# Result banks held as persistent tiles, and a new place for the whole-array blocks among the transpositions

## The chip, the cores and the metric

The kernel runs on one core of a Trainium2 chip. The metric is the device time of one execution in microseconds, the median of several. A ratio is the mean time of one kernel's fast runs over that of the other's of the same rounds, so it is not quite the ratio of the medians that stand beside it.

## The reference

```python
B, S, D, H = 64, 1024, 1024, 16         # Dh = D // H = 64
route_logits = x @ route_w              # (B, S, 16)
best_head = np.argmax(route_logits, axis=-1)
x_heads = x.reshape(B, S, H, Dh)
for h in range(H):
    mask = (best_head == h)
    out[:, :, h, :] = np.matmul(x_heads[:, :, h, :], experts[h]) * mask[:, :, None]
```

Everything is float32. x has 268 MB and out as many: each row is read once and written once, and all but one of its 16 heads is zero in the result.

## The kernel before

The engines are called PE (matrix multiplication; PEld is its loading of weights), ACT, DVE and POOL (work on elements) and SP (which issues loads and stores). SBUF and PSUM are memories on the chip; PE writes its results to banks of PSUM here.

The 65536 rows are cut into 512 tiles of 128 rows, and the loop takes them in pairs. For each tile,

- eight transpositions on PE put x into two PSUM banks (ps_t), four a bank, and ACT copies each bank to SBUF (xt);
- a *split pass* of 40 small matmuls on PE (blocks 0 to 4 of a row, on quarters of the array) writes banks 0 and 1 of a three-bank result tile (ps_e), and ACT copies these two banks to SBUF (raw);
- three *whole-array blocks* (two matmul instructions each) write bank 2 of the same tile;
- DVE reduces the logits out of all three banks, finds the best head, makes the mask, and multiplies bank 2 by it into the output row (ot); POOL multiplies raw by the mask into the rest; SP stores the row.

The kernel holds eight PSUM banks: two for ps_t, and two result tiles of three. A pair's split passes come first; then a string, ORDER, says how the pair's six whole-array blocks (F) are mixed with the 16 transpositions (T) of the next pair.

```python
ORDER = "FTFTFTTTFTFTFTTTTTTTTT"
# ... (cut)
ps_t_pool = ctx.enter_context(tc.tile_pool(name="ps_t", bufs=2, space=bass.MemoryType.PSUM))
ps_e_pool = ctx.enter_context(tc.tile_pool(name="ps_e", bufs=2, space=bass.MemoryType.PSUM))
# ... (cut: constants, load, transposes)

def split_pass(ps, xt):                       # L123: 40 matmuls into banks 0 and 1
    for p in range(NS):
        # ... (cut: half, th)
                    nc.tensor.matmul(ps[th * 64:(th + 1) * 64, half, o0:o0 + W], lhsT=..., rhs=..., ...)
    raw = raw_pool.tile([P, 2, SLOTS * STEP], FP32, name="raw", tag="raw")
    nc.scalar.copy(out=raw[:, :, 0:RW], in_=ps[:, 0:2, 0:RW])        # L130
    return raw

def whole_block(ps, xt, f):                   # L135: bank 2
    nc.tensor.matmul(ps[:, 2, o0:o0 + STEP], lhsT=xt[:, NS + f, :], rhs=mf[:, f, :], ...)

def finish(j, ps, raw):
    parts = ps[:, :, 0:SLOTS * STEP].rearrange("k b (s w) -> k b s w", w=STEP)
    nc.vector.tensor_reduce(out=lg, in_=parts[:, :, :, Dh:W]..., op=ALU.add, axis=AX.XY)   # L142
    # ... (cut: max, max_index, mask)
    nc.vector.tensor_tensor(out=ov[:, NS:], in1=bc(mk[:, NS:]), op=ALU.mult,
                            in0=ps[:, 2, W:W + NF * STEP]...)        # L160, "the multiply"
    # ... (cut: two products on POOL, L168)
    nc.sync.dma_start(out=og[j], in_=ot)

for j in range(-2 * AHEAD, NT + 2, 2):        # manual schedule: engines run in this order
    # ... (cut: loads of 12 tiles ahead)
    pair = [i for i in (j - 2, j - 1) if i >= 0]
    for i in pair:
        ps = ps_e_pool.tile([P, SLOTS, HB], FP32, name="ps_e", tag="ps_e")
        work[i] = (ps, split_pass(ps, xts[i]))
    # ... (cut: tr = the 16 transpositions of tiles j, j + 1)
    for step in order:                        # "T": next(tr); "F": whole_block, and finish
        # ... (cut)                           # after a tile's third
```

## Time and profile before

| | before |
|---|---|
| time, median of 3 | 1503.12 us (1500.57 to 1503.49) |
| PE busy, share of the span | 94% |
| ACT, DVE, POOL busy | 64%, 51%, 48% |
| period: start of one pair's split passes to the next's | 5.75 us median, 5.79 us mean |
| HBM traffic over the span | 359 GB/s |

From the page of the kernel before: busy times of the engines; and of the slices of the span the DMA line (tenths of the time that the DMA engines were busy) and the GB/s they moved.

```profile
PE 1404.1 (94%) x27648; PEld 1231.4 (82%) x27648; DVE 757.4 (51%) x3074; ACT 960.2 (64%) x1537; POOL 721.7 (48%) x1031
...
DMA  9999999999999999999999999999999999999994
GB/s 355 405 365 368 365 367 360 371 369 369 361 361 369 362 371 362 369 360 375 367 365 363 367 367 365 366 360 370 365 361 368 365 363 366 366 368 366 364 350 185
```

The DMA line looks full from start to end, but the GB/s line below it has a slice of 405 among slices of 360 to 375, so busy time is not a measure of what is left. The windows (length in us, busy time and count of each engine, granted clock, DMA share, GB/s) show the same:

```profile
core 0: us, PE busy (x) PEld busy (x) DVE busy (x) ACT busy (x) POOL busy (x), PEclk, DMA share, GB/s
25.00:60.00 35.00, 32.95 (x659) 28.91 (x652) 17.59 (x73) 22.45 (x37) 16.75 (x25) 1.00 1.03 415
300.00:340.00 40.00, 37.63 (x754) 32.98 (x753) 20.20 (x82) 25.67 (x42) 19.71 (x28) 1.00 1.00 372
```

DMA share 1.03 goes with 415 GB/s, and 1.00 with 372. The Trainium skill says it too (Perfetto Trace Analysis, "Identifying the Most-Contended Engine"): for DMA, judge by bandwidth, since 16 engines make occupancy misleading. There was room.

The timeline of one period (start and length in us, engine, line, what, count; in brackets the idle time just before and what ended it):

```profile
700.49 1.89 PE L123 MATMUL ps_e<-mv,xt 64*64 64x80 f32 x80
...
700.76 0.56 DVE L160 TENSOR_TENSOR ot<-ps_e,mask 128x384 f32<-128x384 f32 x1
...
701.43 0.79 PEld L123 LDWEIGHTS ps_e<-mv,xt 64*64 64x64 f32 x40 [0.18 <-ACT xt L114]
...
704.71 0.71 PE L112 MATMUL ps_t<-ident,xin 128*128 128x128 f32 x5
...
705.01 1.08 ACT L114 COPY xt<-ps_t 128x512 f32<-128x512 f32 x2 [0.59 <-PE ps_t L112]
...
705.65 0.66 PE L112 MATMUL ps_t<-ident,xin 128*128 128x128 f32 x4 [0.24 <-ACT xt L114]
```

Two places lose time. The nine transpositions at the end of ORDER are five and then, after a stop, four (705.65): the last four need the ps_t bank whose ACT copy runs from 705.01. And the 80 matmuls of the two split passes, shown as one row, hold a stop at 701.43, where the weight loads (PEld) of the second pass begin. The multiply of the tile that used this ps_e buffer before ends at 701.31 (700.76 and 0.56 are rounded).

The list of waits (us in total, times, longest) blames something else for the second:

```profile
PE ps_t L112 <- ACT xt L114: 64.2, 256, 3.1
...
PEld ps_e L123 <- ACT xt L114: 49.8, 252, 0.5
...
PE ps_t L112 <- DMA xin<-in_x_dram: 4.4, 1, 4.4
```

The second row gives the 49.8 us to an ACT copy. That copy had ended at 701.18, and the semaphore that the waiting instruction names is counted up by DVE: a wait for several semaphores is put down to whichever came last by the profile, and here the profile chose wrongly. The third row is the only wait of PE for a load.

### The profile page before, as it was taken

What the parts mean: (1) busy time and instruction counts of PE and PEld (TensorE: products, weight loads), DVE (VectorE), ACT (ScalarE), POOL (GpSimd) and SP (SyncE); (2) the same over time, 40 slices, a digit from 0 to 9 for tenths busy, and PEclk for the clock granted to TensorE, in tenths of its full rate; (3) what the DMA queues carried; (4) which work ended last, traced back from release to release, by engine and by line L of the source; (5) the groups of instructions that cost most, each with busy time, mean ns of one, the idle gap of its engine ahead of it and who ended that gap; (6) DMA issues with size and microseconds to landing.
All of it is one profiled execution on the core that took longest, in us unless ns stands there. A gap on an engine that the chain in (4) does not pass through costs nothing. (4 is left out here: it accounts for less than half of the span.)

```text
span 1498.0 us, 66591 instructions
## 1 busy us (share of the span) xinstructions
PE 1404.1 (94%) x27648; PEld 1231.4 (82%) x27648; DVE 757.4 (51%) x3074; ACT 960.2 (64%) x1537; POOL 721.7 (48%) x1031
## 2 busy tenths in 40 slices
PE   7999999999999999999999999999999999999997
PEld 6888888888888888888888888888888888888886
DVE  3454545454545555545555555545454545454544
ACT  5666666666666666666666666666666666666665
POOL 3454544444444545444545454545444444444444
PEclk9999999999999999999999999999999999999999
DMA  9999999999999999999999999999999999999994
GB/s 355 405 365 368 365 367 360 371 369 369 361 361 369 362 371 362 369 360 375 367 365 363 367 367 365 366 360 370 365 361 368 365 363 366 366 368 366 364 350 185
DMA packets 149949, 541.52 MB, mean 361 GB/s; under 512 B 18576, under 2 KB 18576, under 8 KB 149648
## 3 DMA queue, kind: packets, MB, share of 16 engines
q1 hardware_dynamic: 147456, 536.94, 96.5%
q8 instruction: 219, 3.59, 1.0%
q10 hardware_dynamic: 2192, 0.33, 0.1%
q14 instruction: 82, 0.67, 0.1%
HBM read 268.76 MB, written 268.44 MB: 359 GB/s over the span
## 5 line engine op out<-in xcount | busy, mean ns | idle before, releaser
L168 POOL TENSOR_TENSOR ot<-raw,mask 128x384 f32<-128x384 f32 (+1 forms) x1024 | 720.9, 725 | 772.1 <-ACT xt L114 682.7
L112 PE MATMUL ps_t<-ident,xin 128*128 128x128 f32 x4096 | 755.5, 277 | 68.6 <-ACT xt L114 64.2
L114 ACT COPY xt<-ps_t 128x512 f32<-128x512 f32 x1024 | 576.9, 587 | 362.7 <-PE ps_t L112 362.4
L112 PEld LDWEIGHTS ps_t<-ident,xin 128*128 128x128 f32 x4096 | 499.6, 141 | 129.3 <-ACT xt L114 124.9
L135 PE MATMUL ps_e<-mf,xt 128*128 128x144 f32 x3072 | 602.1, 296 | 1.0 <-ACT raw L130 0.7
L123 PE MATMUL ps_e<-mv,xt 64*64 64x80 f32 x20480 | 475.9, 234 | 17.3 <-DVE ot L160 4.9
L135 PEld LDWEIGHTS ps_e<-mf,xt 128*128 128x128 f32 x3072 | 462.9, 191 | 34.7 <-ACT raw L130 1.9
L130 ACT COPY raw<-ps_e 128x704 f32<-128x704 f32 x512 | 382.0, 746 | 159.4 <-PE ps_e L123 159.2
L123 PEld LDWEIGHTS ps_e<-mv,xt 64*64 64x64 f32 x20480 | 399.6, 133 | 95.4 <-ACT xt L114 49.8
L142 DVE TENSOR_REDUCE lg<-ps_e 128x16 f32<-128x144 f32 x512 | 155.0, 303 | 624.5 <-PE ps_e L135 616.3
L160 DVE TENSOR_TENSOR ot<-ps_e,mask 128x384 f32<-128x384 f32 x512 | 285.4, 558 | 19.5 <-DVE mask L150 1.5
L150 DVE TENSOR_SCALAR mask<-hid,ix 128x16 f32<-128x16 f32 x512 | 119.9, 234 | 55.9 <-POOL ot L168 1.8
L146 DVE MAX8 mx<-lg 128x8 f32<-128x16 f32 x512 | 91.2, 178 | 17.7
L148 DVE FIND_INDEX8 ix<-mx,lg 128x8 uint32<-128x16 f32 x512 | 86.5, 169 | 0.0
L148 DVE MATCH_VALUE_LOAD ix<-mx,lg 128x8 f32 x512 | 47.1, 92 | 17.6
L114 ACT ACT_TABLE_LOAD x1 | 1.3, 1283 | 7.5 <-DMA mf<-in_experts_dram 7.5
L79 DVE MEMSET mf<- 128x432 f32 x1 | 0.4, 418 | 0.9 <-PEq L220 0.9
masks.py:197 POOL MEMSET ident<- 128x128 f32 x1 | 0.2, 205 | 0.3 <-POOLq L220 0.3
masks.py:199 POOL TENSOR_SCALAR_AFFINE_SELECT ident<-ident 128x128 f32<-128x128 f32 x1 | 0.3, 294 | 0.0
L220 POOL MEMSET const-float32-0.0<- 128x1 f32 x1 | 0.1, 99 | 0.2 <-issue 0.2
L97 POOL IOTA hid_i<- 128x16 int32 x1 | 0.1, 142 | 0.0
L99 DVE CAST hid<-hid_i 128x16 f32<-128x16 int32 x1 | 0.2, 152 | 0.0
(3 smaller groups left out, 0.3 us busy)
## 6 DMA issues: line engine op xcount, KB each, us to landing
xin<-in_x_dram SPq DMA_DIRECT2D x512, 512.0 KB, 7.3
out_dram<-ot SPq DMA_DIRECT2D x512, 512.0 KB, 5.8
mv<-in_experts_dram ACTq DMA_DIRECT2D x2, 48.0 KB, 5.0
mf<-in_experts_dram ACTq DMA_DIRECT2D x2, 48.0 KB, 3.6
mv<-in_experts_dram ACTq DMA_DIRECT2D x2, 32.0 KB, 3.5
mv<-in_route_w_dram ACTq DMA_DIRECT2D x1, 24.0 KB, 4.2
mf<-in_route_w_dram ACTq DMA_DIRECT2D x1, 24.0 KB, 7.5
mv<-in_route_w_dram ACTq DMA_DIRECT2D x1, 16.0 KB, 2.8
```

Of the source, the lines that this page charges most:

```text
L79: nc.vector.memset(mf, 0.0)
L112: nc.tensor.transpose(ps_t[:, q, :], xin[:, p * P:(p + 1) * P], ident)
L114: nc.scalar.copy(out=xt[:, half * (NB // 2):(half + 1) * (NB // 2), :], in_=ps_t)
L123: nc.tensor.matmul(ps[th * 64:(th + 1) * 64, half, o0:o0 + W], lhsT=xt[half * 64:(half + 1) * 64, p, th * 64:(th + 1) * 64], rhs=mv[half * ...
L130: nc.scalar.copy(out=raw[:, :, 0:RW], in_=ps[:, 0:2, 0:RW])
L135: nc.tensor.matmul(ps[:, 2, o0:o0 + STEP], lhsT=xt[:, NS + f, :], rhs=mf[:, f, :], start=(f == 0), stop=(f == NF - 1), skip_group_check=True)
L142: nc.vector.tensor_reduce(out=lg, in_=parts[:, :, :, Dh:W].rearrange("k b s h -> k h b s"), op=ALU.add, axis=AX.XY)
L146: nc.vector.max(out=mx, in_=lg)
L148: nc.vector.max_index(out=ix, in_max=mx, in_values=lg)
L150: nc.vector.tensor_scalar(out=mask, in0=hid, scalar1=ix[:, 0:1], scalar2=None, op0=ALU.is_equal)
L160: nc.vector.tensor_tensor(out=ov[:, NS:], in1=bc(mk[:, NS:]), op=ALU.mult, in0=ps[:, 2, W:W + NF * STEP].rearrange("k (f w) -> k f w", w=S ...
L168: nc.gpsimd.tensor_tensor(out=ov[:, ab:NS:2], in0=rv4[:, 0:n, :, o0:o0 + Dh], in1=bc(mk[:, ab:NS:2]), op=ALU.mult)
```

## The change

The intent: with the result tiles allocated once and used in turn, banks 0 and 1 should become free for the next split pass without waiting for the multiply, which reads bank 2 alone. That should allow the blocks, which delay the multiply when they come late, to move behind the first four transpositions.

```diff
-ORDER = "FTFTFTTTFTFTFTTTTTTTTT"
+ORDER = "TTTTFTFTFTTFTFTFTTTTTT"
@@
-    ps_e_pool = ctx.enter_context(tc.tile_pool(name="ps_e", bufs=2, space=bass.MemoryType.PSUM))
+    ps_e_pool = ctx.enter_context(tc.tile_pool(name="ps_e", bufs=1, space=bass.MemoryType.PSUM))
@@
+    ps_es = [ps_e_pool.tile([P, SLOTS, HB], FP32, name=f"ps_e{i}", tag=f"ps_e{i}") for i in range(2)]
@@
         for i in pair:
-            ps = ps_e_pool.tile([P, SLOTS, HB], FP32, name="ps_e", tag="ps_e")
+            ps = ps_es[i % 2]
             work[i] = (ps, split_pass(ps, xts[i]))
```

## The prediction

> **What bounds it now.** A pair of tiles takes 5.75 us (median distance between starts of the split passes; mean 5.79). The page has PE busy 94%, ACT 64%, DVE 51%, POOL 48%. The slices show DMA at nine tenths all along, but it is not the limit yet: loads run 12 tiles ahead, the waits show PE waiting for one once (4.4 us), and at 25 to 60 us, with a backlog of mixed loads and stores, the windows show 415 GB/s against 372 at 300 to 340 us. PE's in-order chain sets the pace, and loses 0.7 us a period in two places (timeline, 699.9 to 706.3 us):
>
> 1. The last four transpositions wait for a ps_t bank: a gap of 0.51 us instead of 0.11. The eighth transposition comes late (704.71), its ACT copy runs 705.01 to 705.60, PE restarts at 705.65. With the slow restart: 0.45 us.
> 2. The second split pass starts 0.28 us after the first's last matmul instead of 0.02 to 0.05. Its weight load waits for DVE: the multiply out of bank 2 (L160) ends at 701.31, the load starts at 701.43. The waits blame the ACT copy, but that was done at 701.18. 0.25 us.
>
> **What the change does.** No work is added or removed.
>
> Persistent tiles: banks 0 and 1 are free after the ACT copy (0.75 us) and the DVE reduction (0.30), 1.4 us before the end of the multiply, which reads bank 2 alone. Loss 2 should go. The Trainium skill (PSUM — Partial Sum Buffer, "PSUM bank collisions raise a hardware error") asks for guarding by bank and quadrant, so this release is allowed.
>
> Order: four transpositions follow the split pass, while ACT still copies raw. The eighth now stands 1.3 us before the thirteenth (estimate from the spacings 0.109, 0.125 and 0.123 us), over the 0.95 us that copy and restart need. Loss 1 should go. The later blocks delay DVE's second multiply by about 0.8 us; with whole-tile release that would stall the next second split. So the two parts need each other.
>
> PE alone: 5.75 - 0.45 - 0.25 = 5.05 us a period. ACT (3.84), DVE (3.1) and POOL (2.8) fit.
>
> **The new limit.** A period moves 2.10 MB; at 5.05 us that is 415 GB/s, the most this trace showed. The Trainium skill (HBM Reference, "Specifications") gives about 425 GB/s for a core streaming alone. So DMA becomes a second limit: I expect 5.15 to 5.25 us, loads and stores queueing longer, PE sometimes waiting for xin.
>
> 256 x 5.19 us + 22 us (start and end, as now) = about 1350 us, 10% less. Range 1310 to 1420. Faster by over 2%: 0.94; within 2%: 0.04; slower: 0.02.
>
> **What would show it.** PE's idle before transpositions by ACT's xt copy falls from 64 us to under 15; the second split follows the first within 0.05 us; mean rate rises from 361 to about 400 GB/s; landing of a load rises from 7.3 us to 8 to 10; waits of PE for xin appear, if DMA limits.
>
> **What would make it wrong.** The release stays coarse and the split still waits for L160: then the late blocks cost more than they save (1500 or over). DMA sustains less than 400 GB/s over the whole run: packets already took longer at 300 to 340 us than at 25 to 60; at 385 GB/s it would be about 1415.

## More of the kernel before

The programmer writes no semaphore. The framework that builds the program places them, from what each instruction reads and writes of each tile.

## The result

The changed kernel is slower: 1588.09 us (1587.82 to 1590.64, 3 runs) against 1503.12, ratio 1.0575 with a 95% interval of 1.0551 to 1.0600. The result is correct. The median period is 6.10 us instead of 5.75.

Lines shifted by four: transpositions L116, split pass L127, blocks L139, reduction L146, multiply L164. The two result tiles now have names of their own, ps_e_96 for the first of a pair and ps_e_97 for the second. The page:

```profile
PE 1342.4 (85%) x27648; PEld 1222.7 (77%) x27648; DVE 757.1 (48%) x3074; ACT 932.7 (59%) x1537; POOL 720.1 (45%) x1031
...
DMA  9999999999999999999999999999999999999984
GB/s 339 377 348 346 341 352 343 349 344 346 347 345 345 348 342 350 343 348 341 345 345 345 346 344 349 344 350 340 346 343 345 346 346 345 347 345 350 342 323 178
```

PE is busy 85% instead of 94%, and DMA moves 341 GB/s: it waits for the kernel. The windows (same columns as above):

```profile
300.00:340.00 40.00, 33.88 (x722) 30.73 (x723) 20.20 (x82) 23.84 (x40) 19.27 (x28) 1.00 0.94 347
```

The timeline of one period:

```profile
700.19 0.56 DVE L164 TENSOR_TENSOR ot<-ps_e_97,mask 128x384 f32<-128x384 f32 x1
...
700.89 0.92 PE L127 MATMUL ps_e_97<-mv,xt 64*64 64x80 f32 x40 [0.81 <-DVE ot L164]
...
704.38 0.82 PE L116 MATMUL ps_t<-ident,xin 128*128 128x128 f32 x6
...
704.65 0.56 DVE L164 TENSOR_TENSOR ot<-ps_e_96,mask 128x384 f32<-128x384 f32 x1
...
705.12 0.30 DVE L146 TENSOR_REDUCE lg<-ps_e_97 128x16 f32<-128x144 f32 x1
...
705.26 0.92 PE L127 MATMUL ps_e_96<-mv,xt 64*64 64x80 f32 x40
...
706.29 0.56 DVE L164 TENSOR_TENSOR ot<-ps_e_97,mask 128x384 f32<-128x384 f32 x1
```

The six transpositions at the end (704.38) now run without a stop: that loss is gone. But the second split pass, at 700.89, came 0.81 us of idle time late, just after the multiply out of ps_e_97 ended at 700.19 + 0.56 = 700.75. The first split pass, at 705.26, waited for the multiply out of ps_e_96 (it ended at 705.20), although the split pass writes banks 0 and 1 and the multiply reads bank 2. The waits:

```profile
PEld ps_e_97 L127 <- issue: 230.4, 245, 0.9
PE ps_e_97 L127 <- DVE ot L164: 204.0, 250, 1.2
...
PEld ps_e_96 L127 <- DVE ot L164: 78.4, 255, 0.7
```

The first row is the same stop seen by the weight loads, named "issue" because a semaphore instruction of PE's sequencer stands between. The waits for ps_t that cost 64.2 us on PE before are gone; waits for the multiply of 204.0 and 78.4 us have come.

Where the period went, from the distances between starts of successive matmuls in the trace (sums over the run divided by 256 pairs, so the disturbances and the start are in them; us a period):

| from, to | before | changed |
|---|---|---|
| transposition to transposition | 1.57 | 1.06 |
| last transposition to first split pass | 0.20 | 0.34 |
| within the two split passes | 1.70 | 2.44 |
| last split matmul to the next instruction | 0.20 | 0.16 |
| all others with a whole-array block | 2.13 | 2.15 |
| sum | 5.80 | 6.15 |

Loss 1 of the prediction was removed (0.51 us). Loss 2, which should have vanished, grew: the step between the two split passes has a median of 1.04 us instead of 0.28, and the first pass waits 0.13 us too.

### The profile page after: what moved, and what is told of

Same layout as the page of the kernel before. It is cut to its first block, busy times and chain, and to the rows that moved or that the text cites. A ratio compares the mean times of both kernels' runs of the same rounds, so it can differ in the third digit from the quotient of the medians.

```text
span 1586.3 us, 67101 instructions
## 1 busy us (share of the span) xinstructions
PE 1342.4 (85%) x27648; PEld 1222.7 (77%) x27648; DVE 757.1 (48%) x3074; ACT 932.7 (59%) x1537; POOL 720.1 (45%) x1031
## 5 line engine op out<-in xcount | busy, mean ns | idle before, releaser
L116 PE MATMUL ps_t<-ident,xin 128*128 128x128 f32 x4096 | 755.5, 277 | 8.5 <-DMA xin<-in_x_dram 8.3
L116 PEld LDWEIGHTS ps_t<-ident,xin 128*128 128x128 f32 x4096 | 499.1, 141 | 32.5 <-ACT xt L118 4.6
L146 DVE TENSOR_REDUCE lg<-ps_e_96 128x16 f32<-128x144 f32 x256 | 78.9, 308 | 713.0 <-PE ps_e_96 L139 703.8
L127 PE MATMUL ps_e_97<-mv,xt 64*64 64x80 f32 x10240 | 237.1, 234 | 209.0 <-DVE ot L164 204.0
L127 PEld LDWEIGHTS ps_e_97<-mv,xt 64*64 64x64 f32 x10240 | 203.1, 133 | 243.0 <-issue 230.4
L134 ACT COPY raw<-ps_e_97 128x704 f32<-128x704 f32 x256 | 190.8, 745 | 252.6 <-PE ps_e_97 L127 248.7
L139 PE MATMUL ps_e_96<-mf,xt 128*128 128x144 f32 x1536 | 287.8, 287 | 1.5 <-DMA mf<-in_route_w_dram 1.5
L139 PE MATMUL ps_e_97<-mf,xt 128*128 128x144 f32 x1536 | 287.7, 287 | 0.1
L134 ACT COPY raw<-ps_e_96 128x704 f32<-128x704 f32 x256 | 190.7, 745 | 119.3 <-DVE mask L154 115.7
L127 PEld LDWEIGHTS ps_e_96<-mv,xt 64*64 64x64 f32 x10240 | 195.3, 133 | 78.7 <-DVE ot L164 78.4
L127 PE MATMUL ps_e_96<-mv,xt 64*64 64x80 f32 x10240 | 236.8, 235 | 17.8 <-DVE ot L164 2.3
L139 PEld LDWEIGHTS ps_e_96<-mf,xt 128*128 128x128 f32 x1536 | 231.8, 191 | 1.8 <-ACT xt L118 1.7
L139 PEld LDWEIGHTS ps_e_97<-mf,xt 128*128 128x128 f32 x1536 | 231.8, 191 | 0.3 <-ACT raw L134 0.3
L164 DVE TENSOR_TENSOR ot<-ps_e_96,mask 128x384 f32<-128x384 f32 x256 | 142.7, 558 | 9.7 <-DVE mask L154 0.7
L164 DVE TENSOR_TENSOR ot<-ps_e_97,mask 128x384 f32<-128x384 f32 x256 | 142.7, 557 | 9.8 <-DVE mask L154 1.1
L146 DVE TENSOR_REDUCE lg<-ps_e_97 128x16 f32<-128x144 f32 x256 | 76.1, 297 | 0.0
```

Source lines behind the costliest of these rows:

```text
L116: nc.tensor.transpose(ps_t[:, q, :], xin[:, p * P:(p + 1) * P], ident)
L146: nc.vector.tensor_reduce(out=lg, in_=parts[:, :, :, Dh:W].rearrange("k b s h -> k h b s"), op=ALU.add, axis=AX.XY)
```

## The experiments

Theory A: the release is still by whole tile, so the split pass waits for the multiply, and the new order only makes the multiply later. Rival B: the persistent tiles cost time by themselves. Rival C: the new order is dear on PE. "Before" in each row is the kernel before on the same chip in the same rounds.

| run | edit | result | median us | before us | ratio (95% interval) |
|---|---|---|---|---|---|
| e1_order_alone | new order, pool as before | correct | 1587.88 | 1502.41 | 1.0577 (1.0544 to 1.0609) |
| e2_persist_alone | persistent tiles, old order | correct | 1515.23 | 1502.41 | 1.0087 (1.0064 to 1.0109) |
| e3_mult_off_bank | change, multiply reads SBUF | wrong | 1400.65 | 1502.41 | 0.9349 (0.9292 to 0.9406) |
| e4_two_tiles | change, banks as two tiles | correct | 1364.58 | 1502.41 | 0.9086 (0.9061 to 0.9111) |
| e5_two_tiles_old_order | two tiles, old order | correct | 1437.20 | 1503.92 | 0.9552 (0.9531 to 0.9573) |
| e6_two_tiles_pool | two tiles from the pool, new order | correct | 1364.60 | 1503.92 | 0.9083 (0.9052 to 0.9115) |
| e7_half_stores | e4, half of each row stored | wrong | 1339.06 | 1503.92 | 0.8922 (0.8884 to 0.8961) |
| e8_few_stores | e4, every sixteenth tile stored | wrong | 1304.35 | 1503.30 | 0.8680 (0.8665 to 0.8694) |

### The order alone

```diff
 # the kernel before, with
-ORDER = "FTFTFTTTFTFTFTTTTTTTTT"
+ORDER = "TTTTFTFTFTTFTFTFTTTTTT"
```

> The order of the change alone, result banks from the pool as before. Theory A (in the changed kernel the tile is still released as a whole: the second split pass waits for DVE's multiply out of bank 2, and the late blocks delay that multiply): the pool releases whole tiles too, so this must be as slow as the change, 1575 to 1595 us, with the second split pass about 1.1 us after the first. Rival B (the persistent tiles cost the time, through extra semaphore waits on PE and ACT): about 1503 us or less. Rival C (the transition from split pass to transpositions is dear on PE): slow too, but with the loss at that transition and not ahead of the second split pass.

It took 1587.88 us, the time of the whole change; the step between the split passes has a median of 1.04 us, as there, and its waits are those of the change (here a pool of tiles releases them, and the multiply is L160):

```profile
PEld ps_e L123 <- issue: 228.6, 243, 0.9
PE ps_e L123 <- DVE ot L160: 205.8, 257, 1.2
PEld ps_e L123 <- DVE ot L160: 77.7, 254, 0.7
```

So the pool, which gives back a tile as a whole, and the persistent tiles release in the same way. Rival B falls. For rival C: the step from the last split matmul to the first transposition has a median of 0.16 us, below the 0.20 us of the step that it replaces, so the order is not dear by itself.

### The persistent tiles alone

```diff
 # the changed kernel, with
-ORDER = "TTTTFTFTFTTFTFTFTTTTTT"
+ORDER = "FTFTFTTTFTFTFTTTTTTTTT"
```

> The persistent tiles alone, in the old order. Theory A: no release is gained and none lost, 1495 to 1520 us, and the second split pass still waits for the multiply (0.28 us gap as before, or some hundredths more for the added semaphore waits). Rival B: most of the 85 us are here, 1560 us or more. If the release were by bank and the order were to blame, the 0.25 us would be gone: about 1440 us.

It took 1515.23 us, 0.9% more than before: nothing gained, as theory A says. The step between the split passes is 0.27 us (0.28 before). The extra 13 us are mostly in the step from the split pass to the first block, 0.27 us a period instead of 0.20. The waits name ACT's copy of raw there:

```profile
PEld ps_e L139 <- ACT raw L134: 46.7, 234, 0.5
```

The same row of the kernel before:

```profile
PEld ps_e L135 <- ACT raw L130: 1.9, 7, 0.4
```

The first block writes bank 2 and the copy reads banks 0 and 1 of the same tile: the tile is held together in this direction too. (That wait existed before; the copy starts 0.055 us later after the split pass, behind a second semaphore wait of ACT, so that it now comes last.)

The framework can tell why it adds a dependency. Asked for a shortened build of the changed kernel (8 tiles, not run on the chip; `tile_follow` in its tile module prints this), it gave for the first matmul of a split pass into a used tile, in its words and with our names for the instructions:

```
split matmul (banks 0, 1) -> ACT copy of raw   (banks 0, 1):    sync, tensor overlap on 'ps_e0' (WAR)
split matmul (banks 0, 1) -> DVE reduction     (banks 0, 1, 2): sync, tensor overlap on 'ps_e0' (WAR)
split matmul (banks 0, 1) -> DVE multiply      (bank 2 only):   sync, tensor overlap on 'ps_e0' (WAR)
```

The third line is the wait that the change was meant to lose.

### The multiply taken off the bank

```diff
+    fake = consts.tile([P, HB], FP32, name="fake")
+    nc.vector.memset(fake, 1.0)
@@
-            in0=ps[:, 2, W:W + NF * STEP].rearrange(...)
+            in0=fake[:, W:W + NF * STEP].rearrange(...)
```

> The changed kernel, but the DVE multiply reads a constant SBUF tile of the same shape instead of bank 2: wrong result on purpose, same DVE work, and nothing after the reduction holds the banks. Theory A: the wait ahead of the second split pass goes, the period falls from 6.10 to 5.05 to 5.25 us, 1320 to 1370 us. Rivals B and C: the wait is not what costs, so 1540 us or more remain.

It took 1400.65 us. The step between the split passes fell from 1.04 to 0.05 us, and the median period to 4.93 us: the wait for the multiply is what the change lost its time to. The 204.0 and 78.4 us that PE and its weight loads waited for the multiply are gone (0.7 us is left); ahead of the split passes the list of waits has "issue", that is, nothing that the profile names:

```profile
PEld ps_e L129 <- issue: 100.2, 314, 2.2
...
PE ps_e L129 <- issue: 50.5, 72, 2.1
```

The time is 30 us over the expected range, because the mean period is 5.38 us, with long stalls in a few periods (told below, under the stores). The edit was not as neutral as meant either: with both inputs of the multiply in SBUF, POOL's products took 880 ns instead of 723 and DVE's mask 351 ns instead of 234. In the page of this run they are

```profile
L174 POOL TENSOR_TENSOR ot<-raw,mask 128x384 f32<-128x384 f32 (+1 forms) x1024 | 881.9, 880 | 508.4 <-ACT xt L120 435.0
...
L156 DVE TENSOR_SCALAR mask<-hid,ix 128x16 f32<-128x16 f32 x512 | 179.6, 351 | 56.4 <-DVE ix L154 2.4
```

The Trainium skill (SBUF — State Buffer, "SBUF: two separate sides") describes a port pair that a DVE instruction with two SBUF inputs and a GpSimd instruction take from each other for whole instructions. The numbers agree with that: of POOL's two products only the first, which starts 0.1 us after the DVE multiply, is longer (1146 ns instead of 831; the second has 615 in both). No run here isolates it.

### Two tiles for one result

```diff
-    ps_es = [ps_e_pool.tile([P, SLOTS, HB], FP32, name=f"ps_e{i}", tag=f"ps_e{i}") for i in range(2)]
+    ps_es = [(ps_e_pool.tile([P, 2, HB], FP32, name=f"ps_s{i}", tag=f"ps_s{i}"),
+              ps_e_pool.tile([P, 1, HB], FP32, name=f"ps_w{i}", tag=f"ps_w{i}")) for i in range(2)]
@@ split_pass, after the copy of raw: the logits of banks 0 and 1
+        nc.vector.tensor_reduce(out=lga, in_=parts[:, :, :, Dh:W]..., op=ALU.add, axis=AX.XY)
@@ (cut: blocks and multiply index the one bank of the second tile)
@@ finish: the logits of bank 2, and the sum
-        nc.vector.tensor_reduce(out=lg, in_=parts[:, :, :, Dh:W]..., op=ALU.add, axis=AX.XY)
+        nc.vector.tensor_reduce(out=lgb, in_=parts[:, :, Dh:W]..., op=ALU.add, axis=AX.X)
+        nc.vector.tensor_tensor(out=lg, in0=lga, in1=lgb, op=ALU.add)
@@
-            work[i] = (ps, split_pass(ps, xts[i]))
+            work[i] = (ps[1], *split_pass(ps[0], xts[i]))
```

> The changed kernel with banks 0 and 1 as one tile and bank 2 as another, so that they are released apart; the reduction is split in two and an addition is added on DVE (about 0.4 to 0.5 us of DVE work more a tile, an estimate from the 0.30 us of the reduction and 0.18 to 0.23 us of the other DVE instructions of 16 columns). Correct result. Theory A: as the run with the multiply off the bank, 1320 to 1390 us, the longer DVE work being off PE's path; faster than the kernel before by about 10%. If DMA limits: 1390 to 1430 us with PE waiting for xin. If DVE is then the limit: idle of PE ahead of the blocks or split passes by DVE. Rivals B and C: 1540 us or more.

It took 1364.58 us with a correct result: 9.1% less than the kernel before and within the expected range, although DVE works 927 us instead of 757. The timeline of one period (split pass L128, multiply L171, transpositions L117):

```profile
318.02 0.82 PE L117 MATMUL ps_t<-ident,xin 128*128 128x128 f32 x6
...
318.33 0.56 DVE L171 TENSOR_TENSOR ot<-ps_w,mask 128x384 f32<-128x384 f32 x1
...
318.77 1.61 PE L128 MATMUL ps_s<-mv,xt 64*64 64x80 f32 x80
...
320.16 0.56 DVE L171 TENSOR_TENSOR ot<-ps_w,mask 128x384 f32<-128x384 f32 x1
...
320.31 0.66 PE L117 MATMUL ps_t<-ident,xin 128*128 128x128 f32 x4
```

The 80 matmuls of both split passes start at 318.77 and run through in 1.61 us, while the two multiplies end at 318.89 and 320.72: 0.12 and 1.2 us after the passes that would have waited for them had begun (the second began at 319.51). The step between the passes has a median of 0.05 us, as in the run with the multiply off the bank. The undisturbed period is 4.93 us. The mean is 5.24 us; where those 0.31 us are is told below.

### Two tiles in the old order

```diff
 # e4_two_tiles, with
-ORDER = "TTTTFTFTFTTFTFTFTTTTTT"
+ORDER = "FTFTFTTTFTFTFTTTTTTTTT"
```

> Two tiles a result (banks 0 and 1, bank 2) with the order of before. It separates the two losses of the prediction. If they are independent, the second split pass follows at once (0.05 us instead of 0.28) and the wait for the ps_t bank stays: 5.75 - 0.23 + 0.06 (what the persistent tiles alone cost) = about 5.58 us a period, 1430 to 1460 us. If the release alone makes the gain of the run with two tiles: 1365 us. If it is worth nothing without the order: 1500 us.

It took 1437.20 us, 4.5% less than before: the step between the split passes is gone, and the stop for the ps_t bank stays, 64.1 us where the kernel before has 64.2:

```profile
PE ps_t L117 <- ACT xt L119: 64.1, 256, 3.2
```

So the early release is worth about 67 us by itself, the order by itself costs 85 us, and both together gain 138 us: the order needs the release, as the prediction said, but the change had no release to give it.

### Two tiles without persistence

```diff
 # e4_two_tiles, with bufs=2 in ps_e_pool, no ps_es, and in the loop
-            ps = ps_es[i % 2]
+            ps = (ps_e_pool.tile([P, 2, HB], FP32, name="ps_s", tag="ps_s"),
+                  ps_e_pool.tile([P, 1, HB], FP32, name="ps_w", tag="ps_w"))
```

> Two tiles a result and the new order, but taken from a rotating pool again, not persistent. If the cut into two tiles does it all and persistence nothing: 1345 to 1370 us, no slower than the persistent form, with 512 instructions fewer on PE. If persistence were needed for the early release: over 1450 us.

It took 1364.60 us, as long as the persistent form (ratios 0.9083 and 0.9086). The early release comes from the cut into two tiles; persistence adds nothing to it. The expected saving of 512 instructions on PE was wrong: PE has 775 semaphore instructions here and 774 with persistent tiles.

### What limits the version with two tiles

In that run the windows show

```profile
300.00:340.00 40.00, 39.30 (x816) 36.68 (x818) 27.63 (x123) 27.69 (x47) 20.88 (x31) 1.00 1.03 413
```

DMA moved 413 GB/s, the rate at which it worked off the backlog in the kernel before. The Trainium skill (HBM Reference, "Specifications") gives about 425 GB/s for a core that streams alone; loads and stores mixed reached 413 to 415 here. The undisturbed period of 4.93 us would need 2.10 MB / 4.93 us = 426 GB/s. So DMA stands near the most that these traces show, but it does not hold PE up in the way that was predicted:

```profile
PEld ps_s L128 <- issue: 97.1, 326, 1.6
...
PE ps_s L128 <- issue: 44.2, 68, 1.5
...
PE ps_t L117 <- DMA xin<-in_x_dram: 4.3, 1, 4.3
```

PE waited for a load (xin) once. From the twentieth tile on, loads landed 15.9 us or more before their first use. Instead PE stops in the middle of its work, with nothing to wait for ("issue"), as at 304.91, where a split pass is broken after 70 of 80 matmuls:

```profile
302.99 1.47 PE L128 MATMUL ps_s<-mv,xt 64*64 64x80 f32 x70
...
304.91 0.49 PE L128 MATMUL ps_s<-mv,xt 64*64 64x80 f32 x10 [0.46 <-issue]
```

Counted in the trace, 66 steps between successive matmuls are longer than 0.56 us after the first 20 us of the run. All 66 lie at one place modulo 256 in the order of PE's weight loads, matmuls and semaphore instructions (within two instructions), and each ends 2.2 to 2.9 us (median 2.3) after a packet of 16384 bytes of the instruction queue started. (219 such packets came; PE's 56073 instructions make 219 lines of 256.) The Trainium skill (Advanced Engine Details and Errata, "ISA Cache") gives a line of 16 KB, 256 instructions. A period has about 219 of these instructions, so PE needs a new line every 5.8 us on average (6.7 us in the kernel before). The packets of all 66 stalls had started 3.4 us or more after the last edge; 37 packets as late brought no step of over 0.56 us; the time from edge to edge varies from 5.2 to 7.2 us, which may be why. The median start was 3.3 us after the edge (2.2 us in the kernel before). To see whether DMA traffic makes the packets late, two runs took stores away.

```diff
 # e7_half_stores
-        nc.sync.dma_start(out=og[j], in_=ot)
+        nc.sync.dma_start(out=og[j][:, 0:D // 2], in_=ot[:, 0:D // 2])
 # e8_few_stores
+        if j % 16 == 0 or j >= NT - 2:
             nc.sync.dma_start(out=og[j], in_=ot)
```

> The kernel with two tiles and the new order, storing only the left half of each result row: wrong result on purpose, a quarter of the DMA bytes less, everything else the same. In the run with two tiles PE's undisturbed period was 4.93 us, which would need 426 GB/s, while the windows showed 405 to 413 GB/s; the mean period was 5.24 us, and all 66 stalls of over 0.56 us fell on multiples of 256 instructions of PE, the 16 KB of one instruction-fetch packet. Theory: fetches come late because DMA is full. Then with a quarter less traffic the stalls go and the mean period is 4.93 to 4.98 us, 1280 to 1300 us. If the stalls are PE's own fetch cost at this pace, they stay: about 1360 us.

> The kernel with two tiles and the new order, storing only every sixteenth result: wrong result on purpose, DMA carries loads and little else. With half of each store left out, the stalls at multiples of 256 instructions fell from 66 to 36 only, and the time to 1339 us. Two readings: (a) fetches start late by what DMA has queued (median 3.3 us after PE passed the last block's edge in the run with two tiles, 2.5 us with half stores); with almost no stores the delay falls below 2 us, stalls of over 0.56 us to under 10, and the time to 1275 to 1295 us, the undisturbed 4.93 us a period. (b) At 5.7 us for 256 instructions PE outruns its fetches whatever DMA carries: stalls and time stay near 36 and 1335 us.

The windows from 300 to 340 us, half stores and then few stores:

```profile
300.00:340.00 40.00, 40.00 (x868) 37.86 (x868) 29.04 (x130) 28.78 (x48) 22.49 (x32) 1.00 0.91 319
```

```profile
300.00:340.00 40.00, 39.59 (x865) 37.35 (x864) 28.81 (x128) 28.78 (x48) 22.50 (x32) 1.00 0.61 226
```

| | e4_two_tiles | e7_half_stores | e8_few_stores |
|---|---|---|---|
| DMA, MB in all | 542 | 407 | 291 |
| median us from a line's edge to its packet's start | 3.3 | 2.5 | 2.1 |
| stalls over 0.56 us after 20 us | 66 | 36 | 15 |
| sum over periods of what exceeds the median of 4.93 us | 80 us | 56 us | 22 us |
| time, us | 1364.58 | 1339.06 | 1304.35 |

(The three ran on different chips, on which the kernel before took 1502.41, 1503.92 and 1503.30 us.) Of the 80, 56 and 22 us in the fourth row, about 70, 46 and 18 us are at the edges of lines, counted in the traces as what each step takes over its median. The first of the two runs missed its expectation (1280 to 1300 us), and the second missed it by 9 us, but the direction is clear: with the traffic falls the lateness of the packets, and with it most of the stalls. Traffic is not all of it: the kernel before, at 361 GB/s but with a longer period, had its packets at 2.2 us, earlier than half stores at 305 GB/s (2.5 us). Reading (b), that PE outruns its fetches whatever DMA carries, is not borne out; but a pace of 4.93 us leaves so little slack that some stalls remain even at 226 GB/s. What delays the packets within DMA is open. So is why the run with the multiply off the bank had longer stalls (77 of them, 88 us in all, at the same places) than the run with two tiles (66 and 62 us) at about the same traffic (388 and 398 GB/s). One part is known: four times in mid-run its granted clock fell to 0.5 for 3.41 us, each within 2 us after a PE stall of over 2 us (three other such stalls were not followed by one); at half speed that is at most 1.7 us each, or 7 us in all (an estimate), of the 36 us between the two runs. In the profile of the run with two tiles the clock fell only at the end.

## Why the prediction was wrong

- **The step that failed** is "Persistent tiles: banks 0 and 1 are free after the ACT copy (0.75 us) and the DVE reduction (0.30), 1.4 us before the end of the multiply, which reads bank 2 alone. Loss 2 should go." The runs show that the release of the persistent tile is by whole tile, as from the pool: the second split pass waits for the multiply (1.04 us step), the order alone costs the same 85 us as the change, and two tiles give the time that was predicted. I took a statement of the change's intent, and what would be safe by banks, for what the program's semaphores do. The Trainium skill (PSUM — Partial Sum Buffer, "PSUM bank collisions raise a hardware error") says what must be guarded, by bank and quadrant; it does not say that a program guards no more than that. The trace of before could not show this, as both causes of the wait are the same semaphore of DVE there.
- **What would make it wrong** was named: "The release stays coarse and the split still waits for L160: then the late blocks cost more than they save (1500 or over)." This is what happened. The chance given to it, 0.06 for "same" and "slower" together, was far too small for a thing that had not been checked.
- **Loss 1** was right: the stop for the ps_t bank is gone in the changed kernel (transposition to transposition 1.06 us a period instead of 1.57).
- **"So the two parts need each other"** was right, and cut the other way: order alone +85 us, release alone -67 us, both -138 us.
- **PE alone, 5.05 us a period**: 4.93 us where the release is real. By medians of the run with two tiles against the kernel before, loss 1 was worth 0.51 us instead of 0.45, loss 2 0.28 instead of 0.25, and the step after the split passes became 0.04 us shorter (0.16 instead of 0.20); the steps with blocks stayed (2.14 and 2.13).
- **The new limit** came out right in size in the version with two tiles (5.24 us mean period, 413 GB/s, loads landing in 8.5 us instead of 7.3), but partly by luck: PE alone took 0.12 us less than said, and what came on top was 0.31 us instead of 0.10 to 0.20. Its form was wrong: PE does not wait for xin; it stalls at instruction-line edges, and the stalls fell from 66 to 15 when the stores were taken away.

## What to carry to other kernels

Before you count on an early release, ask the framework which instructions it makes the next writer wait for (the semaphore alone was not enough here: reduction and multiply count up the same one), or give what must be released apart a tile of its own. Here the cut into two tiles was worth 4.5% in the old order and 9.1% with the new one, with an added reduction and addition, and persistence nothing. A reordering that makes a consumer later needs the early release first, or it turns the gain into a longer wait. When PE runs almost without gaps and DMA carries much, look for stalls with no wait named, not only for late loads: there were 36 of them even at 305 GB/s.

## What the Trainium skill lacked or had wrong

- PSUM — Partial Sum Buffer: it gives the rule for guarding by bank, but not that a tile over several banks can be guarded as a whole by the framework, which costs what bank-wise release would gain: 1588 us with one three-bank tile, 1365 us with the banks as two tiles.
- Runtime: NRT & Kernel Launch, "Instruction fetch mechanics": it says that an engine fetches its next block of 256 instructions over a DMA queue, and that the cost of crossing a block is "mostly hidden". In the kernel before that fits (3 us at the edges of lines); with the shorter period it does not: about 70 us of 1365 us at 398 GB/s, about 18 us of 1304 us at 223 GB/s (the mean rates of the two runs), all stalls of over 0.56 us at multiples of 256 instructions. Advanced Engine Details and Errata, "ISA Cache", gives the line of 256 instructions without a cost.
- HBM Reference, "Specifications": about 425 GB/s for a core alone; 413 to 415 GB/s for half loads and half stores here, so no contradiction, but no page that we used has the figure for mixed traffic.
